# Attention in a hybrid decoder layer: q projected from consecutive tokens and transposed straight into place, inverse roots by Ln, Exp and one Newton step

## The chip, the cores and the metric

The kernel runs on one core of one Trainium2 chip. The metric is the device time of one execution in microseconds; the kernel before has three runs, and their median is 2185.88 us. The engines are named as in the profile: PE is TensorE (PEld its weight loads), DVE is VectorE, ACT is ScalarE, POOL is GpSimd, and SP is SyncE, which here only issues DMAs.

## The reference, cut to what matters

One decoder layer over x of 2048 tokens by 1024 in float32. Eight attention heads of 64, each with three dilated windows whose results are mixed by their softmax denominators; a short convolution stands beside them; a SwiGLU follows.

```
h = rms_norm(x, g_mix);  z = h @ w_in
u, gb, gc, q, k, v = split(z)
y_conv = gb * short_conv(gc * u, conv_w)
q = rms_norm(q.reshape(B, S, 8, 64), g_q) * 64 ** -0.5
k = rms_norm(k.reshape(B, S, 8, 64), g_k)
y_attn = dilated_mixture(q, k, v)        # (window, dilation) = (128,1), (512,4), (2048,16)
mix = concat(rms_norm(y_conv), rms_norm(y_attn));  x = x + mix @ w_out
h = rms_norm(x, g_ffn);  x = x + (silu(h @ w_gate) * (h @ w_up)) @ w_down
```

The normalisation of q and k is what the change touches: each of 64 elements is multiplied by 1/sqrt(mean of squares + 1e-6).

## The kernel before, in words

Every matrix product is made in three float16 products, high by high, high by low and low by high, because each float32 operand is split into a high and a low half (mm3_steps, L182 to L190: three matmuls per chunk k of 128 contraction rows, eight chunks). The stages are: the input norm and three quarters of the convolution (in_and_conv), attention (attention_pairs), the output projection (out_b), the feed-forward (ffn).

Attention works on four pairs of heads, g = 0 to 3. For each pair, qkv_steps (L443 to L507) projects q, k and v of both heads, in blocks of 512 tokens (i), four tiles of 128 tokens (j) each. A tile takes every fourth token of its block (t = slice(j, 4 * P, 4), L461), as the layout of k and v wants it. The tile's matmuls have the tokens as stationary operand and 384 columns of weights moving: 128 of q, 128 of k, 128 of v. ACT copies q and k out of PSUM (L468), squares them (L469), and splits v with DVE (L472, L473). When four tiles are there, DVE sums the squares (L479) and makes the inverse root of 128x16 numbers by rsqrt (L39 to L51): a shift and a subtraction on the bits of the number as a first guess (L45, L46), three Newton rounds of three operations (L48 to L50), and a multiplication by 2^11 (L482). POOL multiplies q and k by it (L483, L486); ACT and POOL split them in high and low halves in one buffer, qkhl (L492 to L495). SP issues three transposing DMAs of 128x1024 (L499 to L502): one for q into the scratch qp, two for k into ka and kl. Since the tokens of a tile are four apart, DVE copies q from qp into token order in qT (L503 to L505), one copy of 128x512 per head.

attn_steps (L509 to L651) runs the three branches of both heads over qT, ka and kl: matmuls of q against k in high and low (L606, L607), mask and row minimum on DVE (L612), Exp on ACT (L617), a split into halves (L627, L628), a transposing DMA of the weights (L629) or, where only one block of keys is seen, a transposition on PE (L622 to L624), and the product with v (L635). POOL combines the three branches of a head (combine, L536 to L559).

What sets the order: attention_pairs (L707 to L727) weaves the projection of pair g+1, or in the last pair the remaining quarter of the convolution and the first part of the output projection (tail_steps), between the steps of attention g, so many projection steps per attention step (rate) and not before the product with v some steps back (lag, issue_after). A projection step is one yield: three matmuls, or the end of a block. The framework then orders the instructions of each engine by a simulated timeline and puts in all semaphores. Each engine, and SP's queue of DMAs, works in that order, so an instruction that waits holds all behind it. The first pair's projection (qkv_steps(0)) has no attention beside it until its first block is done.

Buffers: the pool qk has four buffers of 4 KB per partition under the name qT. Two are used for the heads of a pair; in the convolution they serve as w1 (L301), in the input norm for tiles 6 and 7 (L393), in the output projection (out_a, L781) for the residual tiles x1 of two rows of tokens, where p is not 1, 4 or 7. The names ka and kb have two buffers of 8 KB each.

Of the kernel before, what the change touches and what calls it, by code (L numbers as in the profile page):

```python
# [2 lines left out]

# [5 lines left out]
F32 = mybir.dt.float32  # L9
F16 = mybir.dt.float16  # L10
I32 = mybir.dt.int32
AF = mybir.ActivationFunctionType
ALU = mybir.AluOpType
# [4 lines left out]
P = 128  # L18
S = 2048
D = 1024  # L20
# [5 lines left out]
HD = 64  # L26
EPS = 1e-6


class Builder:  # L30
# [167 lines left out]
    def run(self):  # L198
        tc, nc, A = self.tc, self.nc, self.A
        with ExitStack() as ctx:  # L200
            cp = ctx.enter_context(tc.tile_pool(name="const", bufs=1))
            self.cp = cp
            dr = self.dr = ctx.enter_context(tc.tile_pool(name="dram", bufs=1, space=DRAM))
            self.d_ya = dr.tile([P, 4, S], F32, name="d_ya")
            self.d_v = [dr.tile([2, S, 2 * HD + 2], F16, name=f"d_v{g}") for g in range(4)]
            self.d_u = [[dr.tile([S, HD + 2], F32, name=f"d_u{h}_{b}") for b in range(2)] for h in range(H)]
            self.d_wq = [dr.tile([P, 2, KC, 384], F16, name=f"d_wq{g}") for g in range(5)]
            self.d_wo = [dr.tile([P, 2, KC, 512], F16, name=f"d_wo{g}") for g in range(2)]
            self.d_y = dr.tile([S, 512], F32, name="d_y")
            self.d_x1 = dr.tile([S, D], F32, name="d_x1")  # L210
            self.d_h = dr.tile([S // 2, 7, 2 * 512], F16, name="d_h")
            self.d_wd = [dr.tile([P, NF // 2, 2, 512], F16, name=f"d_wd{n}") for n in range(7)]
            self.d_a = dr.tile([P, NF, S], F32, name="d_a")

            self.ident32 = cp.tile([P, P], F32, name="ident32")
            self.ones = cp.tile([P, 1], F32, name="ones")
            self.eps = cp.tile([P, 3], F32, name="eps")
            self.wsm = ctx.enter_context(tc.tile_pool(name="wsm", bufs=3))
            self.big = ctx.enter_context(tc.tile_pool(name="big", bufs=1))
            self.wq = ctx.enter_context(tc.tile_pool(name="wq", bufs=2))  # L220
            with ExitStack() as c1:
                e = c1.enter_context
                self.psmm = e(tc.tile_pool(name="psmm", bufs=3, space=PSUM))
                self.qk = e(tc.tile_pool(name="qk", bufs=4))
                self.mixer(c1)

                self.fs = ctx.enter_context(tc.tile_pool(name="fs", bufs=1, side="right"))
                self.fw = ctx.enter_context(tc.tile_pool(name="fw", bufs=15, side="right"))

                self.gs = ctx.enter_context(tc.tile_pool(name="gs", bufs=2, side="right"))  # L230
                self.psg = ctx.enter_context(tc.tile_pool(name="psg", bufs=4, space=PSUM, side="right"))
                self.out_b()
            self.ffn()
# [36 lines left out]
    def conv_steps(self, j, W, before=None, scratch=None):  # L270


        nc, wc = self.nc, self.wc
        NC = 512
        prev = None
        two = {}
# [6 lines left out]
        for c in range(S // NC):  # L283
            if before:
                before(c)
            t = slice(c * NC, (c + 1) * NC)
# [11 lines left out]
                return ps, u  # L298
            gc, u = yield from gemm(2)
            own = scratch if c == 0 else None  # L300
            w1 = own[:, 0:2] if own is not None else self.qk.tile([P, 2, NC], F32, name="qT")  # L301
            gcs, a = w1[:, 0], w1[:, 1]
            nc.scalar.activation(gcs, gc, AF.Copy, scale=u)
            yield True
# [14 lines left out]
            y, s2 = w2[:, 0], w2[:, 1]  # L319
# [5 lines left out]
            acc = self.sq[:, c] if j < 3 else s2  # L325
            if j == 0:
                s2 = acc
            nc.scalar.activation(s2, y, AF.Square)
            if 0 < j < 3:
                nc.gpsimd.tensor_tensor(acc, acc, s2, op=ALU.add)  # L330
                s2 = acc
# [33 lines left out]
    def in_and_conv(self):  # L365
        tc, nc, A = self.tc, self.nc, self.A
        w_in, w_out = A["w_in"][0], A["w_out"][0]
        with ExitStack() as c:
# [21 lines left out]
                W[m] = self.weights([cols(0)[m]], ux, dst=(t0[:, 0, :, cs], t0[:, 1, :, cs]), raw=raw0[:, m])  # L390

            def norm(i, n):
                tags = 6 * ("nx_x",) + ("qT", "qT") + 8 * ("nx_x",)  # L393
                self.norm(i, [(self.qk if tg != "nx_x" else xp).tile([P, D], F32, name=tg) for tg in tags[i:i + n]],
                          [t[:, j] for tg in ("ka", "kb")[i % 4 // 2:(i % 4 + n) // 2]
                           for t in (self.qk.tile([P, 2, 2, D], F16, name=tg, bufs=2),) for j in range(2)])
            spills = []
# [45 lines left out]
    def qkv_steps(self, g, st):  # L443
# [5 lines left out]
        u = self.uq[:, g:g + 1]  # L449
        st["u"] = u  # L450
        yield
        qT = [self.qk.tile([P, S], F16, name="qT") for _ in range(2)]

        ka, kl = (self.qk.tile([P, 4, 2, 512], F16, name=nm, bufs=2) for nm in ("ka", "kb"))
        dv = self.d_v[g]
        for i in range(0, NT, 4):
            f = self.at.tile([P, 4, 4, HD], F32, name="qkf", bufs=2)
            for j in range(4):
                vs = self.vs[i // 4 % 2]

                t = slice(j, 4 * P, 4)  # L461
                xh, xl = self.x[i // 4]
                ps = self.psmm.tile([P, 512], F32, name="mm")
                yield from self.mm3_steps(ps[:, 0:384], lambda k: xh[:, k, t], lambda k: xl[:, k, t],
                                          lambda k: wh[:, k], lambda k: wl[:, k])
                if j == 0:
                    n = self.at.tile([P, 16, HD], F32, name="qkn")
                nc.scalar.activation(f[:, j].rearrange("p a b -> p (a b)"), ps[:, 0:256], AF.Copy, scale=u)  # L468
# [8 lines left out]
            ff = f.rearrange("p a b d -> p (a b) d")  # L477
            ss = self.at.tile([P, 16], F32, name="qk_ss")
            nc.vector.tensor_reduce(ss, n, axis=AX.X, op=ALU.add)  # L479
            nc.vector.tensor_scalar(ss, ss, 1.0 / HD, EPS, op0=ALU.mult, op1=ALU.add)  # L480
            r = self.rsqrt(self.at, ss, 16, "qkr")
            nc.vector.tensor_scalar_mul(r, r, 2.0 ** 11)  # L482
            nc.gpsimd.tensor_tensor(n, ff, r.unsqueeze(2).broadcast_to([P, 16, HD]), op=ALU.mult)  # L483
            n4 = n.rearrange("p (a b) d -> p a b d", a=4)
            nk = n4[:, :, 2:4]
# [9 lines left out]
                nc.gpsimd.tensor_tensor(hl[:, 4 + h, :, 0], k, hl[:, 2 + h, :, 0], op=ALU.subtract)  # L495


            qp = self.at.tile([P, 2, 4, P], F16, name="qp", bufs=2)
            for n_, dst in enumerate((qp, ka[:, i // 4].rearrange("p h (j t) -> p h j t", j=4),  # L499
                                      kl[:, i // 4].rearrange("p h (j t) -> p h j t", j=4))):  # L500
                self.transpose(dst.rearrange("p h j t -> p (h j) t"),
                               hl[:, 2 * n_:2 * n_ + 2].rearrange("p h j x d -> p (h j x d)"))  # L502
            for h in range(2):  # L503
                nc.vector.tensor_copy(qT[h][:, i * P:(i + 4) * P].rearrange("p (t j) -> p t j", j=4),
                                      qp[:, h].rearrange("p j t -> p t j"))  # L505
            yield
        st.update(qT=qT, ka=ka, kl=kl)  # L507

    def attn_steps(self, g, st):  # L509
# [16 lines left out]
                for r in range(4):  # L526
                    nc.sync.dma_start(t[32 * r:32 * r + 32], dv.rearrange("(n p r) c -> r p n c", n=NT, r=4)[r])
        for h, b in [(h, b) for h in range(2) for b in (1, 2, 0)]:
            qT = st["qT"][h]
            ka, kl = (st[x][:, :, h] for x in ("ka", "kl"))  # L530
            load_v(h, b)

# [134 lines left out]
    def attention_pairs(self):  # L667
# [27 lines left out]
        nc.vector.tensor_scalar_mul(self.kap, u, HD ** -0.5 * 2.0 ** -22)  # L695
        nc.vector.tensor_scalar_mul(self.nkap, self.kap, -1.0)

        self.qkhl = self.at.tile([P, 6, 4, 2, HD], F16, name="qkhl")
        nc.gpsimd.memset(self.qkhl[:, 4:6, :, 1], 0.0)
        self.y7 = self.rows.tile([P, NT, HD], F32, name="y7")  # L700
# [61 lines left out]
    def out_a(self, p):  # L762
# [5 lines left out]
            ya = tk[:, 0].rearrange("p a (b c) -> p (a b) c", c=2 * P).rearrange("p k (j t) -> p k j t", j=2)  # L768
        else:
            ya = self.op.tile([P, 4, 2, P], F32, name="ya")  # L770
        xk = self.qk.tile([P, 2, D], F32, name="kb", bufs=2) if p % 3 == 1 else None
        for j in range(2):
            nc.sync.dma_start(ya[:, :, j], self.d_ya[:, :, (p + 8 * j) * P:(p + 8 * j + 1) * P])
        for k in range(4):
# [3 lines left out]
        self.x1[p] = []  # L778
        for j in range(2):
            i = p + 8 * j  # L780
            x1 = self.qk.tile([P, D], F32, name="qT") if xk is None else xk[:, j]  # L781
            nc.sync.dma_start(x1, self.A["x"][0][i * P:(i + 1) * P])
            t = tk[:, 1, j] if p < 2 else self.op.tile([P, 512], F32, name="xt", bufs=2)

# [436 lines left out]
```

## Time and profile before

| what | value |
|---|---|
| three runs | 2181.43, 2185.88, 2189.73 us; median 2185.88 |
| span of the profiled execution | 2189.4 us; the run of 2189.73 is the one that fits it, 0.3 around the span |
| PE busy over the span | 2068.8 us, 94% |
| DVE, ACT, POOL busy | 1457.8 (67%), 1025.1 (47%), 625.8 us (29%) |
| mean granted clock of PE | 0.984 |
| loads of ACT's function table | 5 |

Matmuls are pipelined, so PE counts as busy also where the next one starts only as the last one's results arrive; what a matmul costs is read from the distance of two starts, not from its length. A row of a timeline gives start, length, engine, line, operation, the tile written and those read, the shape, and in brackets the idle time before it and what ended it. A row of waits gives who waited, for whom, the microseconds in total, how often, and the longest. A row of groups gives busy time, the mean in ns, and the idle time before.

### The profile page before, as it was taken

The page shows a single profiled execution, that of the slowest core. Times are in us where ns is not written, and L with a number is a line of the kernel's source. Part 1 is how long each engine was busy: PE and PEld are TensorE (multiplying, and loading weights), DVE is VectorE, ACT ScalarE, POOL GpSimd, SP SyncE. Part 2 cuts the span into 40 slices and gives each one's busy share as a digit, 9 for nine tenths or more (in the row PEclk, how much of TensorE's full clock was granted, in tenths as well). Part 3 has the DMA queues.
Part 4 walks back from the last instruction along what each step waited for, and adds up shares of the span by engine and source line. Part 5 has one row for each costly group of instructions (what it writes and reads, how often), then busy time and mean ns, then how long its engine had stood idle before and what let it go on. Part 6 is the DMA issues. An engine that isn't in the chain of part 4 may idle for free. (4 is left out here: it accounts for less than half of the span.)

```text
span 2189.4 us, 32832 instructions
## 1 busy us (share of the span) xinstructions
PE 2068.8 (94%) x11864; PEld 1077.2 (49%) x11864; DVE 1457.8 (67%) x3380; ACT 1025.1 (47%) x2134; POOL 625.8 (29%) x515
## 2 busy tenths in 40 slices
PE   4899999989899889999999999999999999999999
PEld 2344567767666544443444444444444444444444
DVE  5687446778776687795767676756676666545554
ACT  6443346776766656563433333333333334444341
POOL 0000133343443212120232111211121145555463
PEclk9999999999999989999999999999999999999999
DMA  9767458899989996799332233223322663251342
GB/s 245 169 201 243 115 119 153 186 178 178 183 168 202 208 214 216 242 276 263 124 109 87 97 106 101 89 95 101 106 87 97 235 241 105 77 180 54 119 142 96
DMA packets 555492, 339.64 MB, mean 155 GB/s; under 512 B 354624, under 2 KB 508224, under 8 KB 552896
## 3 DMA queue, kind: packets, MB, share of 16 engines
q1 hardware_dynamic: 537648, 314.38, 55.9%
q10 hardware_dynamic: 17680, 23.16, 3.0%
q8 instruction: 93, 1.52, 0.3%
q14 instruction: 71, 0.58, 0.1%
HBM read 161.24 MB, written 107.54 MB: 123 GB/s over the span
## 5 line engine op out<-in xcount | busy, mean ns | idle before, releaser
L1001 PEld LDWEIGHTS <-w 128*128 128x128 f16 x3696 | 362.3, 98 | 454.9 <-issue 20.2
L1001 PE MATMUL ps<-b,w 128*128 128x512 f16 x2112 | 466.5, 382 | 14.0 <-DVE s L1007 6.1
L1132 PE MATMUL ps<-b,w 128*128 128x512 f16 x1848 | 399.8, 379 | 4.0 <-DVE s L1153 2.2
L1001 PE MATMUL ps<-hb,w 128*128 128x512 f16 x1584 | 347.1, 379 | 0.0
L1132 PEld LDWEIGHTS <-w 128*128 128x128 f16 x1848 | 180.8, 98 | 222.9 <-issue 5.4
L187 PE MATMUL mm<-wq,b 128*128 128x384 f16 x512 | 171.8, 335 | 7.1 <-DVE vs L473 7.1
L894 POOL TENSOR_TENSOR t<-wq 128x512 f32<-128x512 f32 (+1 forms) x46 | 59.5, 1294 | 411.4 <-issue 239.0
L1007 DVE TENSOR_TENSOR s<-ps,s 128x512 f32<-128x512 f32 x220 | 150.0, 683 | 34.4 <-PE ps L1001 33.9
L189 PE MATMUL mm<-wq,b 128*128 128x384 f16 x512 | 171.7, 335 | 0.0
L188 PE MATMUL mm<-wq,b 128*128 128x384 f16 x512 | 171.5, 335 | 0.0
L1139 POOL TENSOR_TENSOR x<-x,s 128x512 f32<-128x512 f32 x72 | 103.4, 1436 | 172.6 <-DVE s L1153 134.2
L1140 DVE SCALAR_TENSOR_TENSOR x<-ps,a_u,x 128x512 f32<-128x512 f32 x96 | 71.8, 749 | 100.9 <-PE ps L1132 74.3
L617 ACT ACTIVATE s<-s,u 128x256 f32<-128x256 f32 (+1 forms) x224 | 97.9, 452 | 69.4 <-DVE u L612 50.2
L612 DVE CUSTOM_DVE_ANT_0 s<-s,mask,nkap 128x256 f32<-128x256 f32 (+1 forms) x224 | 104.6, 483 | 19.5 <-PE s L607 13.9
L188 PEld LDWEIGHTS <-b 128*128 128x128 f16 x768 | 84.5, 110 | 67.1 <-issue 18.2
L187 PEld LDWEIGHTS <-b 128*128 128x128 f16 x768 | 84.4, 110 | 61.5 <-ACT b L775 6.4
L911 ACT CAST w<-t 128x512 f16<-128x512 f32 x88 | 53.7, 616 | 127.4 <-PE ps L1001 61.9
L189 PEld LDWEIGHTS <-b 128*128 128x128 f16 x768 | 84.2, 110 | 57.2 <-issue 5.2
L187 PE MATMUL cvx<-b,wq 128*128 128x512 f16 (+1 forms) x200 | 77.0, 388 | 32.1 <-ACT kb L264 24.8
L635 PE MATMUL av<-v,et 128*128 128x65 f16 x1800 | 77.7, 195 | 28.1 <-DMA et<-eh 18.7
L606 PE MATMUL s<-ka,qT 128*128 128x128 f16 (+1 forms) x408 | 91.8, 272 | 10.3 <-DVE eh L628 9.2
L1120 DVE TENSOR_TENSOR w<-t,w 128x512 f16<-128x512 f32 (+1 forms) x96 | 75.3, 801 | 34.2 <-ACT w L1119 33.9
(297 smaller groups left out, 3773.4 us busy)
## 6 DMA issues: line engine op xcount, KB each, us to landing
d_a<-a ACTq DMA_DIRECT2D x88, 256.0 KB, 2.0
d_wd<-w SPq DMA_DIRECT2D x77, 256.0 KB, 2.1
wq<-d_a SPq DMA_DIRECT2D x64, 256.0 KB, 4.2
b<-d_wd SPq DMA_DIRECT2D x14, 1024.0 KB, 6.3
wraw<-in_w_in_dram SPq DMA_DIRECT2D x24, 512.0 KB, 7.2
d_h<-hl SPq DMA_DIRECT2D x24, 512.0 KB, 3.2
wq<-in_w_gate_dram SPq DMA_DIRECT2D x22, 512.0 KB, 5.3
wq<-in_w_up_dram SPq DMA_DIRECT2D x22, 512.0 KB, 5.2
```

What stands on the lines that cost most here:

```text
L187: self.pe = mm(ps, lhsT=lh(k), rhs=rh(k), start=k == ks[0], stop=False)
L188: mm(ps, lhsT=lh(k), rhs=rl(k), start=False, stop=False)
L189: mm(ps, lhsT=ll(k), rhs=rh(k), start=False, stop=k == ks[-1])
L606: nc.tensor.matmul(o, lhsT=query(u), rhs=hi[x], start=True, stop=False)
L612: nc.vector.tensor_tensor_reduce(sm[:, at[u]], sp[:, at[u]], mask[:, P - P * has_prev(u):256], accum_out=Ub[:, u, HD + 1:HD + 2], op0=ALU.add,
L617: nc.scalar.activation(sm[:, at[u]], sm[:, at[u]], AF.Exp, scale=-1.0, bias=Ub[:, u, HD + 1:HD + 2])
L635: self.pe_av = nc.tensor.matmul(av[:, u - u0], lhsT=p_, rhs=v_, start=n_ == 0, stop=n_ == len(ops) - 1)
L1001: nc.tensor.matmul(ps[self.BANK[n]], lhsT=w[:, x, k], rhs=b[:, y, k], start=first and k == 0 and q == 0, stop=k == 3 and q == 2, skip_grou ...
L1007: nc.vector.tensor_tensor(t, x, y, op=ALU.add)
L1120: nc.vector.tensor_tensor(L[n][:, 1, 0:n_f], src[n], L[n][:, 0, 0:n_f], op=ALU.subtract)
L1132: nc.tensor.matmul(ps[self.BANK[n]], lhsT=L[n][:, x, f], rhs=B[n][:, f, y], start=first and f == 0 and q == 0, stop=f == n_f - 1 and q == ...
L1139: nc.gpsimd.tensor_tensor(o, o, s_, op=ALU.add)
```

## The change

Five edits. (1) A tile's k and v are still projected from every fourth token, with 256 columns moving; q is projected by 24 matmuls of its own, of 128 columns, from 128 consecutive tokens, into the same PSUM tile and without yields between them. (2) Its transposes, one per head and of half the size, go straight into qT; the scratch qp and DVE's copies are gone. (3) The inverse root comes from Ln and Exp on ACT and one Newton round on DVE. (4) The table set that has Ln and Exp is loaded after the last square of the third convolution quarter. (5) The qT buffers become two of 8 KB, each for both heads, or for pairs of the other uses.

```diff
-                self.qk = e(tc.tile_pool(name="qk", bufs=4))
+                self.qk = e(tc.tile_pool(name="qk", bufs=2))
...
-            w1 = own[:, 0:2] if own is not None else self.qk.tile([P, 2, NC], F32, name="qT")
+            w1 = own[:, 0:2] if own is not None else pair(c, "qT").rearrange("p (a b) -> p a b", a=2)
...
-        qT = [self.qk.tile([P, S], F16, name="qT") for _ in range(2)]
-
+        qT = self.qk.tile([P, 2, S], F16, name="qT")
...
-                t = slice(j, 4 * P, 4)
                 xh, xl = self.x[i // 4]
                 ps = self.psmm.tile([P, 512], F32, name="mm")
-                yield from self.mm3_steps(ps[:, 0:384], lambda k: xh[:, k, t], lambda k: xl[:, k, t],
-                                          lambda k: wh[:, k], lambda k: wl[:, k])
+                t, tq = slice(j, 4 * P, 4), slice(j * P, (j + 1) * P)
+                yield from self.mm3_steps(ps[:, 128:384], lambda k: xh[:, k, t], lambda k: xl[:, k, t],
+                                          lambda k: wh[:, k, 128:384], lambda k: wl[:, k, 128:384])
+                self.mm3(ps[:, 0:128], lambda k: xh[:, k, tq], lambda k: xl[:, k, tq],
+                         lambda k: wh[:, k, 0:128], lambda k: wl[:, k, 0:128])
...
+            r = self.at.tile([P, 16], F32, name="qkr_y")
+            t = self.at.tile([P, 16], F32, name="qkr_t")
+            nc.scalar.activation(t, ss, AF.Ln, scale=1.0 / HD, bias=self.lnb[:, 0:1])
+            nc.scalar.activation(r, t, AF.Exp, scale=-0.5, bias=self.lnb[:, 1:2])
             nc.vector.tensor_scalar(ss, ss, 1.0 / HD, EPS, op0=ALU.mult, op1=ALU.add)
-            r = self.rsqrt(self.at, ss, 16, "qkr")
-            nc.vector.tensor_scalar_mul(r, r, 2.0 ** 11)
+            nc.vector.scalar_tensor_tensor(t, r, -0.5 * 2.0 ** -22, r, op0=ALU.mult, op1=ALU.mult)
+            nc.vector.tensor_tensor(t, t, ss, op=ALU.mult)
+            nc.vector.scalar_tensor_tensor(r, t, 1.5, r, op0=ALU.add, op1=ALU.mult)
...
-            qp = self.at.tile([P, 2, 4, P], F16, name="qp", bufs=2)
-            for n_, dst in enumerate((qp, ka[:, i // 4].rearrange("p h (j t) -> p h j t", j=4),
-                                      kl[:, i // 4].rearrange("p h (j t) -> p h j t", j=4))):
-                self.transpose(dst.rearrange("p h j t -> p (h j) t"),
+            for h in range(2):
+                self.transpose(qT[:, h, i * P:(i + 4) * P].rearrange("p (j t) -> p j t", j=4),
+                               hl[:, h].rearrange("p j x d -> p (j x d)"))
+            for n_, dst in ((1, ka), (2, kl)):
+                self.transpose(dst[:, i // 4].rearrange("p h (j t) -> p (h j) t", j=4),
                                hl[:, 2 * n_:2 * n_ + 2].rearrange("p h j x d -> p (h j x d)"))
-            for h in range(2):
-                nc.vector.tensor_copy(qT[h][:, i * P:(i + 4) * P].rearrange("p (t j) -> p t j", j=4),
-                                      qp[:, h].rearrange("p j t -> p t j"))
...
+        with self.tc.issue_after(self.sqr.ins):
+            nc.scalar.preload_act_table_set("natural_log_exp_and_others")
+        self.lnb = self.at.tile([P, 2], F32, name="lnb")
+        nc.vector.memset(self.lnb[:, 0:1], EPS)
+        nc.vector.memset(self.lnb[:, 1:2], 11 * math.log(2.0))
...
-        xk = self.qk.tile([P, 2, D], F32, name="kb", bufs=2) if p % 3 == 1 else None
+        xk = self.qk.tile([P, 2, D], F32, name="kb" if p % 3 == 1 else "qT")
...
-            x1 = self.qk.tile([P, D], F32, name="qT") if xk is None else xk[:, j]
+            x1 = xk[:, j]
```

The lines left out give the last square of the convolution a name (self.sqr, L328), give the input norm's tiles 6 and 7 one buffer, and let the attention read its head's half of qT.

More of the change, by code (lines that the diff above doesn't have):

```diff
@@ L2 @@
 from itertools import chain, islice
+import math
 import concourse.bass as bass
@@ L327, in conv_steps @@
                 s2 = acc
-            nc.scalar.activation(s2, y, AF.Square)
+            self.sqr = nc.scalar.activation(s2, y, AF.Square)
             if 0 < j < 3:
@@ L392, in norm @@
             def norm(i, n):
-                tags = 6 * ("nx_x",) + ("qT", "qT") + 8 * ("nx_x",)
-                self.norm(i, [(self.qk if tg != "nx_x" else xp).tile([P, D], F32, name=tg) for tg in tags[i:i + n]],
+                two = self.qk.tile([P, 2, D], F32, name="qT") if i <= 6 < i + n else None
+                self.norm(i, [two[:, k - 6] if k in (6, 7) else xp.tile([P, D], F32, name="nx_x") for k in range(i, i + n)],
                           [t[:, j] for tg in ("ka", "kb")[i % 4 // 2:(i % 4 + n) // 2]
@@ L528, in attn_steps @@
         for h, b in [(h, b) for h in range(2) for b in (1, 2, 0)]:
-            qT = st["qT"][h]
+            qT = st["qT"][:, h]
             ka, kl = (st[x][:, :, h] for x in ("ka", "kl"))
```

## The prediction

> **What bounds the kernel now.** I read the table of stages first, then the chain of waits by engine, then the timeline around each wait that TensorE (PE) has in the attention stage.
>
> ```profile
> 307.00:690.00 383.00, 349.60 (x3383) 263.20 (x3382) 280.87 (x1009) 259.06 (x693) 148.73 (x115) 0.96 0.92 179
> ...
> 1045.00:2189.00 1144.00, 1130.89 (x5230) 511.29 (x5228) 722.67 (x1237) 430.01 (x764) 382.28 (x299) 1.00 0.35 116
> ```
>
> The columns are stretch, length, busy time of PE, of PE's weight loads, of DVE, ACT and POOL, granted clock, DMA share, GB/s. The feed-forward stage, 1144 us from 1045 on, has PE busy for 1130.89 and is not touched. The change acts in the 383 us from 307 to 690, where attention of one pair of heads runs beside the projection of the next; the first projection stands ahead of it. PE is busy there for 349.60, so at most some 33 us can be won from waiting. Who ends these waits:
>
> ```profile
> PE s L606 <- DVE eh L628: 8.9, 6, 2.6
> PE av L635 <- DMA et<-eh: 7.9, 12, 2.0
> PE mm L187 <- DVE vs L473: 6.9, 5, 2.2
> ```
>
> ```profile
> DVE qT L504 <- DMA qp<-qkhl: 15.8, 9, 5.9
> ```
>
> Eleven waits, 15.8 us, are for DVE. Another 7.9 us are for the DMA transposes of the softmax weights. DVE, in its turn, stood for 15.8 us in front of the copy of q (L504), with everything queued behind it.
>
> **What the change removes: the copy.** The timeline where PE waited for DVE (the brackets hold the idle time before the instruction):
>
> ```profile
> 617.67 4.92 DVE L504 COPY qT<-qp 128x512 f16<-128x512 f16 x2 [0.19 <-DMA qp<-qkhl]
> ...
> 623.65 0.37 PE L606 MATMUL s<-ka,qT 128*128 128x256 f16 x1 [2.57 <-DVE eh L628]
> ```
>
> ```profile
> 353.23 0.32 PE L187 MATMUL mm<-wq,b 128*128 128x384 f16 x1 [0.55 <-DVE vs L473]
> ...
> 429.49 0.32 PE L187 MATMUL mm<-wq,b 128*128 128x384 f16 x1 [1.12 <-DVE vs L473]
> ...
> 504.33 0.37 PE L606 MATMUL s<-ka,qT 128*128 128x256 f16 x1 [2.14 <-DVE eh L628]
> ...
> 562.89 0.27 PE L606 MATMUL s<-ka,qT 128*128 128x256 f16 x1 [0.74 <-DVE eh L628]
> ```
>
> Followed back step by step, each of these five stalls leads over the softmax's DVE and ACT steps, or over L473 alone, to a copy L504. At 617.67 two copies took 4.92 us, against 29.9 us for all 32 (below). The five stalls are 0.55 + 1.12 + 2.14 + 0.74 + 2.57 = 7.1 us. The copies go, and nothing else was queued before those DVE steps, so I take all of it: **-7.1 us**; between -4 (the next late transpose takes over) and -7.1.
>
> **What the change removes: the root's DVE steps.**
>
> ```profile
> L504 DVE COPY qT<-qp 128x512 f16<-128x512 f16 x32 | 29.9, 976 | 19.3 <-DMA qp<-qkhl 19.2
> ...
> L50 DVE SCALAR_TENSOR_TENSOR qkr_y<-qkr_t,qkr_y 128x16 f32<-128x16 f32 x48 | 10.6, 222 | 1.1
> ```
>
> ```profile
> 569.29 2.16 DVE L46 TENSOR_SCALAR qkr_y<-qkr_i 128x16 int32<-128x16 int32 x1
> ...
> 572.80 0.28 PE L606 MATMUL s<-ka,qT 128*128 128x128 f16 x1 [2.45 <-DVE eh L628]
> ```
>
> ```profile
> 448.45 0.53 PE L635 MATMUL av<-v,et 128*128 128x65 f16 x12 [1.81 <-ACT u L638]
> ```
>
> Thirteen DVE operations of 128x16 per block of 512 tokens become four: L45, L46, two of three rounds of L48 to L50 and L482 go. At L50's mean of 0.222 us, nine are 2.0 us per block, 32 us over the 16 blocks, and the copies are 29.9: 62 us of DVE time, which costs PE only where DVE is late. Two stalls, 2.45 + 1.81 = 4.3 us, lead back to such a step drawn out to about 2 us (L46 at 569.29 is one; why, the rows don't say). Four steps stay that can be drawn out likewise, so I take half: **-2.2 us**, between 0 and -4.3.
>
> **What it adds on PE.** Each of the 64 tiles had 24 matmuls of 384 columns; it gets 24 of 256 and 24 of 128, each with a weight load of its own: 1536 more. Starts in one stretch:
>
> ```profile
> 435.34 0.22 PE L607 MATMUL s<-kb,qT 128*128 128x128 f16 x1
> 435.40 0.27 PE L606 MATMUL s<-ka,qT 128*128 128x256 f16 x1
> 435.50 0.27 PE L607 MATMUL s<-kb,qT 128*128 128x256 f16 x1
> 435.61 0.27 PE L606 MATMUL s<-ka,qT 128*128 128x256 f16 x1
> ...
> 435.83 0.33 PE L187 MATMUL mm<-wq,b 128*128 128x384 f16 x1
> 436.00 0.33 PE L188 MATMUL mm<-wq,b 128*128 128x384 f16 x1
> ```
>
> ```profile
> 402.31 0.30 PE L607 MATMUL s<-kb,qT 128*128 128x128 f16 x1
> 402.44 0.30 PE L606 MATMUL s<-ka,qT 128*128 128x128 f16 x1
> ```
>
> From start to start: 384 columns take about 0.163 us, 256 take 0.108, 128 take about 0.056 where the moving operand is contiguous (435.34) and 0.13 where both operands step (402.31). All had their weight load hidden or paid within that. The new q matmuls have both operands contiguous, and the stationary tokens of k and v step by four as qT does at 435.34, so I take the first: 0.108 + 0.056 - 0.163 = 0.001 to 0.002 us, times 1536: **+2.5 us**. The bounds are -1 (rounding) and 1536 x 0.074 = +114.
>
> The Trainium skill, "TensorE: Matmul & The Clock Gate", section "Back-to-back issue gap", speaks against the change: it puts a sustained stream of weight load and 128-column matmul at about 81 ns each, which would make this term 1536 x 0.026 = 40 us, an estimate from that page. The rows from 435.34 on do not agree; they stand in short runs, though, and the new ones are runs of 24.
>
> **What it adds on SP's queue.** Three transposes per block become four, the two of q half as large.
>
> ```profile
> L195 SPq DMA_TRANSPOSE qp<-qkhl x16: 1232/1292/2314, 268.7 to 667.1; - x16
> ```
>
> Issuing one took SP 1.29 us in the median. Twelve of the 16 blocks lie beside attention: 12 x 1.29 = 15.5 us more of SP in 383. Queued behind are the transposes of the softmax weights, for which PE already waits. Half size may be cheaper to issue; no row shows it. If one in three lands on a transpose that PE waits for, it is +5; freed DVE writes those weights earlier, up to -8. I take **+1**.
>
> **What it adds on ACT.** Ln and Exp on 128x16, nearest:
>
> ```profile
> L546 ACT ACTIVATE cw<-cw 128x48 f32<-128x48 f32 (+1 forms) x11 | 2.7, 241 | 8.5 <-DVE cw L545 8.4
> ```
>
> ```profile
> 286.85 1.28 ACT L617 ACT_TABLE_LOAD   x1
> ```
>
> 2 x 0.24 x 12 = 5.8 us on an engine busy 259.06 of 383; that alone is hidden by its idle time. But Ln waits on ACT for DVE's sum, DVE's next step waits for Exp, and ACT's evacuations and exponentials queue behind Ln, as DVE's masks queue behind that step: **+1**, 0 to +12. The table load, 1.28 us once, moves ahead of attention, where PE had other work: 0.
>
> **What the paired buffers add.** Two buffers of 8 KB replace four of 4 KB. The orders of reuse come out equal, but both halves of a pair are released together.
>
> ```profile
> 888.09 1.14 ACT L858 ACTIVATE ka<-qT,n_y 128x1024 f32<-128x1024 f32 x1
> ...
> 894.94 0.59 PE L187 MATMUL mm<-b,b 128*128 128x512 f16 x1 [4.29 <-DVE qT L788]
> ```
>
> In the output stage a load of x into such a buffer waits for L858; the first half now waits for the second's 1.14 us as well, at three places, of which one stalls PE today: **+1.1**, 0 to +3.4.
>
> The sum: -7.1 - 2.2 + 2.5 + 1 + 1 + 1.1 = **-3.7 us**. The profiled span is 2189.4; one of the three runs is 2189.73, 0.3 around it, and the median of the three, 2185.88, is 3.5 below the span. So 2185.7 for such an execution, **2182 us** for the median.
>
> **Rivals.** Half a percent, 11 us, is about what a measurement of this kernel can tell from no change.
>
> First, DVE's relief reaches the transposes too. For it: 62 us less on DVE, and DVE feeds every transpose. Against: several of those stalls lead back to PE itself and to a long transfer. With all 11.4 us of the DVE stalls and the 7.9 us for the transposes gone, and the costs of 5.6: -13.7 us, so 2172. Chance 0.29.
>
> Second, slower: the wait for the copy comes back as the round trip to ACT. Place: DVE's step behind Exp, and ACT behind Ln, in 12 blocks. The old wait of 15.8 us and copies of up to 29.9 cost PE 7.1, some 0.2 us for each us that DVE stood or copied. ACT and DVE now stand both; with 2.5 us each per block, 60 us in all, PE loses 12: 2182 + 12 = 2194. It passes 2197, and so decides, from about 3.2 us per block. ACT's longest such wait is in the row below, its mean 1.5.
>
> ```profile
> ACT s L617 <- DVE u L612: 43.9, 29, 5.7
> ```
>
> Chance 0.09.
>
> Third, slower: weight loads set the pace of the 128-column matmuls. At midway between 0.056 and 0.13 it is 1536 x 0.037 = 57 us, and 2182 + 57 = 2239; it decides from 0.066 us a matmul. Chance 0.04; the page's 81 ns lies in this case.
>
> Fourth, the change doesn't do what it says: Ln and Exp do not share the loaded table set, and each block loads twice, 32 x 1.28 = 41 us on ACT, some 16 us at PE: 2198. The Trainium skill, "ScalarE: Activation LUTs", section "Table sets: the hidden batching unit", has both functions in the set that is named; no run here shows it yet. Chance 0.03.
>
> **How the numbers follow.** Within 0.5%: 0.55, with an own range from 2175, where the DVE stalls go whole and the costs are near zero, to 2193, where ACT's term is at its end. Faster: 0.29, the first rival. Slower: 0.16, the last three, 0.09 + 0.04 + 0.03. The range leaves out about 0.1 on either side: from 2165 (the first rival with the terms of ACT, SP and the buffers at zero, 2169, less half the 8 us over which the three runs spread) to 2198 (the second at 2.5 us, 2194, and the same half; the table loads give as much).
>
> **What would show it.** Right: no wait of DVE for q's transposes; the five stalls gone; 128-column L187 to L189 starting 0.056 apart; five table loads; PE's waits for transposes as before. Wrong: DVE waiting for ACT at the Newton step or ACT at Ln by over 3 us a block; q's matmuls over 0.066 apart; SP's longer queue showing as more waits for the softmax transposes; or these waits shrinking by more than half.

## The result, and the profile after

| kernel | median of its four runs | ratio to before, 95% interval |
|---|---|---|
| before | 2186.85 us (2181.43 to 2189.73) | 1 |
| the change | 2173.64 us (2171.84 to 2177.16) | 0.9944 [0.9929, 0.9959] |

The change is 13.2 us faster. The interval lies wholly below 1, so there is a gain; whether it is more or less than 0.5% is not settled, as 0.995 lies inside the interval. The forecast was 2182 us; the result lies inside its range, and next to the 2172 us of its first rival.

The profiled execution has a span of 2170.0 us (the run of 2171.84) against 2189.4. The table of stages of the changed kernel, over the stretch of attention that was shown of before, and a stretch of the feed-forward as long as the one shown:

```profile
307.00:690.00 383.00, 355.44 (x4677) 328.91 (x4676) 249.02 (x901) 274.54 (x740) 149.69 (x115) 1.00 0.97 187
...
1026.00:2170.00 1144.00, 1134.72 (x5252) 513.60 (x5249) 724.65 (x1238) 429.85 (x764) 382.38 (x299) 1.00 0.35 117
```

The feed-forward is as it was. In attention the DVE column fell from 280.87 to 249.02 us, and the granted clock, 0.96 before, is 1.00. To see all of attention, here is the stretch from its first product with v to its last, 479.4 us before:

```profile
323.90:803.30 479.40, 435.01 (x4212) 317.92 (x4212) 355.90 (x1307) 316.83 (x841) 160.55 (x119) 0.95 0.94 186
```

and 460.3 us after:

```profile
323.10:783.40 460.30, 425.25 (x5317) 370.93 (x5317) 311.71 (x1167) 326.00 (x874) 157.08 (x118) 0.98 0.98 192
```

The 19.1 us between these two are the whole difference of the two spans, 19.4. PE idled 479.40 - 435.01 = 44.4 us before and 460.30 - 425.25 = 35.1 us after: 9.3 us. The other 9.8 us are busy time of PE, although it runs 1105 matmuls more; the granted clock beside them is 0.98 where it was 0.95. Who ended PE's waits in the first stretch of the changed kernel, and the one wait of ACT that the change added:

```profile
PE av L640 <- DMA et<-eh: 17.8, 21, 2.5
...
PE s L611 <- DVE eh L633: 2.5, 5, 1.0
```

```profile
ACT qkr_t L484 <- DVE qk_ss L481: 7.0, 6, 1.5
```

The waits for DVE, 8.9 + 6.9 us before, are down to 2.5, and the longest is 1.0. But the wait of the product with v for the transposed softmax weights has grown from 7.9 to 17.8 us, where "as before" was forecast. Part of that is the stretch, which ends at 690 us in both kernels, while the changed one is further on by then: over all of attention, 307 to 790 us, the two are 18.7 and 22.7 us (the rows stand under e1 and e2).

The new operations, from the table of groups (busy us, mean ns, idle before):

```profile
L485 ACT ACTIVATE qkr_y<-qkr_t,lnb 128x16 f32<-128x16 f32 x16 | 5.1, 322 | 0.4
L484 ACT ACTIVATE qkr_t<-qk_ss,lnb 128x16 f32<-128x16 f32 x16 | 5.1, 321 | 10.6 <-DVE qk_ss L481 10.4
L487 DVE SCALAR_TENSOR_TENSOR qkr_t<-qkr_y 128x16 f32<-128x16 f32 x16 | 4.0, 247 | 0.7 <-ACT qkr_y L485 0.7
```

the q matmuls of one tile, the first two and the last of 24, and the next tile's first matmul of k and v, from PE's timeline:

```profile
349.62 0.22 PE L188 MATMUL mm<-wq,b 128*128 128x128 f16 x1
349.68 0.22 PE L189 MATMUL mm<-wq,b 128*128 128x128 f16 x1
...
350.91 0.22 PE L190 MATMUL mm<-wq,b 128*128 128x128 f16 x1
350.96 0.27 PE L188 MATMUL mm<-wq,b 128*128 128x256 f16 x1
```

and q's transposes on SP's queue (minimum, median and maximum ns of issuing one):

```profile
L196 SPq DMA_TRANSPOSE qT<-qkhl x32: 1188/1223/2569, 270.8 to 664.1; - x32
```

### The profile page after: what moved, and what is told of

Its sections match the earlier page's. It is cut to its first block, busy times and chain, and to the rows that moved or that the text cites. A ratio compares the mean times of both kernels' runs of the same rounds, so it can differ in the third digit from the quotient of the medians.

```text
span 2170.0 us, 35813 instructions
## 1 busy us (share of the span) xinstructions
PE 2063.9 (95%) x13400; PEld 1153.8 (53%) x13400; DVE 1407.3 (65%) x3206; ACT 1033.2 (48%) x2166; POOL 626.2 (29%) x515
## 4 chain that ended last, share of the span: by engine, by line
PE 44%; DVE 2%; DMA 2%; ACT 1%; POOL 1%; issue 1%; SPq 0%; ACTq 0%; DVEq 0%; POOLq 0%
PE ps L1011 29%; PE ps L1142 15%; DMA wq<-d_a 1%; ACT wq L1120 0%; DVE w L1130 0%; ACT wq L941 0%; DVE w L922 0%; DMA wq<-in_w_up_dram 0%; DMA wq<-in_w_gate_dram 0%; POOL x L1149 0%; ACT w L1129 0%; DVE s L1017 0%; POOL t L904 0%; DVE w L925 0%; DMA wq<-in_w_down_dram 0%
## 5 line engine op out<-in xcount | busy, mean ns | idle before, releaser
L1011 PEld LDWEIGHTS <-w 128*128 128x128 f16 x3696 | 362.6, 98 | 452.8 <-issue 17.4
L1011 PE MATMUL ps<-b,w 128*128 128x512 f16 x2112 | 466.4, 381 | 12.3 <-DMA b<-d_h 4.6
L189 PE MATMUL mm<-wq,b 128*128 128x256 f16 (+1 forms) x1024 | 233.7, 248 | 0.0
L188 PE MATMUL mm<-wq,b 128*128 128x256 f16 (+1 forms) x1024 | 231.5, 248 | 0.0
L190 PE MATMUL mm<-wq,b 128*128 128x256 f16 (+1 forms) x1024 | 231.3, 248 | 0.0
L189 PEld LDWEIGHTS <-b 128*128 128x128 f16 x1280 | 134.4, 105 | 36.6 <-issue 5.9
L188 PEld LDWEIGHTS <-b 128*128 128x128 f16 x1280 | 134.3, 105 | 36.6 <-ACT b L785 4.9
L190 PEld LDWEIGHTS <-b 128*128 128x128 f16 x1280 | 134.1, 105 | 31.6 <-issue 0.8
L622 ACT ACTIVATE s<-s,u 128x256 f32<-128x256 f32 (+1 forms) x224 | 98.8, 456 | 28.8 <-DVE u L617 20.0
L640 PE MATMUL av<-v,et 128*128 128x65 f16 x1800 | 80.3, 195 | 27.1 <-DMA et<-eh 22.7
L633 DVE TENSOR_TENSOR eh<-s,eh 128x512 f16<-128x512 f32 (+1 forms) x112 | 75.2, 678 | 42.3 <-ACT eh L632 42.1
L1043 ACT ACTIVATE sg<-s,w_un 128x512 f32<-128x512 f32 x66 | 47.2, 719 | 105.2 <-DVE s L1017 105.2
```

What stands on the lines that cost most here:

```text
L188: self.pe = mm(ps, lhsT=lh(k), rhs=rh(k), start=k == ks[0], stop=False)
L189: mm(ps, lhsT=lh(k), rhs=rl(k), start=False, stop=False)
L190: mm(ps, lhsT=ll(k), rhs=rh(k), start=False, stop=k == ks[-1])
L622: nc.scalar.activation(sm[:, at[u]], sm[:, at[u]], AF.Exp, scale=-1.0, bias=Ub[:, u, HD + 1:HD + 2])
L633: nc.vector.tensor_tensor(eh[:, w:2 * w], sm[:, 0:w], eh[:, 0:w], op=ALU.subtract)
L640: self.pe_av = nc.tensor.matmul(av[:, u - u0], lhsT=p_, rhs=v_, start=n_ == 0, stop=n_ == len(ops) - 1)
```

## The experiments

Twelve kernels ran. Ratios are against the kernel before on the same chip; its medians there were 2185.87 us for the first four, 2187.15 for the next four, 2186.38 for the three after, and 2186.57 for the last.

| kernel | median us | ratio, 95% interval | DVE busy us |
|---|---|---|---|
| e1 q part alone | 2203.12 | 1.0078 [1.0065, 1.0091] | 1437.9 |
| e2 root alone | 2173.59 | 0.9943 [0.9926, 0.9960] | 1425.7 |
| e3 change, q in one stream with k and v | 2174.34 | 0.9944 [0.9931, 0.9957] | 1407.2 |
| e4 change, q's matmuls spread | 2184.00 | 0.9987 [0.9973, 1.0000] | 1412.9 |
| e5 before, later order | 2195.32 | 1.0048 [1.0025, 1.0071] | 1458.0 |
| e6 change, later order | 2191.59 | 1.0034 [1.0018, 1.0051] | 1406.8 |
| e7 q part alone, later order | 2202.02 | 1.0069 [1.0044, 1.0093] | 1435.6 |
| e8 root alone, later order | 2176.08 | 0.9958 [0.9939, 0.9978] | 1423.5 |
| e9 root alone and nine idle DVE steps | 2196.34 | 1.0057 [1.0036, 1.0078] | 1492.6 |
| e10 before, q transposed by head | 2182.08 | 0.9980 [0.9965, 0.9996] | 1453.1 |
| e11 change with two waiting copies | 2191.56 | 1.0023 [1.0010, 1.0036] | 1453.7 |
| e12 change with two copies that don't wait | 2192.26 | 1.0022 [1.0008, 1.0036] | 1458.8 |

The first theory, C, was that the copy of q and DVE's wait in front of it were most of the gain. Its rivals, as they came up: D, that DVE's occupied time is what counts, whichever step fills it; T, that the shorter chain from the sum of squares to POOL's multiplication counts; S, that the fourth transpose on SP's queue takes something back. The texts put on record before the runs name some others: R, that the root is the gain; W and L, that the added matmuls or their standing in one lump are what the q part pays; O, that the order of the instructions moves the time as much as the change does, against M, that it doesn't.

**The two parts alone (e1, e2).** e1 is the kernel before with edits 1, 2 and 5 of the change (q projected apart, transposed by head, no copy, paired buffers) and the old root. e2 is the kernel before with edits 3 and 4 alone:

```diff
+            nc.scalar.activation(t, ss, AF.Ln, scale=1.0 / HD, bias=self.lnb[:, 0:1])
+            nc.scalar.activation(r, t, AF.Exp, scale=-0.5, bias=self.lnb[:, 1:2])
...
-            r = self.rsqrt(self.at, ss, 16, "qkr")
-            nc.vector.tensor_scalar_mul(r, r, 2.0 ** 11)
+            nc.vector.scalar_tensor_tensor(t, r, -0.5 * 2.0 ** -22, r, op0=ALU.mult, op1=ALU.mult)
+            nc.vector.tensor_tensor(t, t, ss, op=ALU.mult)
+            nc.vector.scalar_tensor_tensor(r, t, 1.5, r, op0=ALU.add, op1=ALU.mult)
```

> The q part of the change alone (own matmuls for q, transposes straight into qT, no copy, paired buffers), with the inverse root made on DVE as before. Theory C (the copy with its wait for the transpose held DVE, and most of the gain is that DVE is free of it): most of the 13 us, 2175 to 2179, no wait of DVE for q's transposes, few of PE for L628 and L473. Rival R (the shorter root is what counts, the copy was hidden): 2183 or more.

> The root part alone (Ln, Exp, one Newton round, the table loaded ahead), with q projected beside k and v, transposed into the scratch and copied as before. Theory C: 2182 to 2187, DVE still waits some 15 us for q's transposes. Rival R: 2176 to 2180. A third possibility, that the two only help together because either alone leaves DVE late: both e1 and e2 at 2182 or more.

Theory C fell at once, and R held in kind, though e2 is faster than R's 2176 to 2180. The root alone gives the whole gain, 0.9943; the q part alone, with no copy and no wait in front of it, is 17 us slower than before. PE's waits over all of attention (307 to 790 us), first of before:

```profile
PE av L635 <- DMA et<-eh: 18.7, 19, 3.0
PE s L606 <- DVE eh L628: 9.2, 7, 2.6
PE mm L187 <- DVE vs L473: 6.9, 5, 2.2
```

of the q part alone:

```profile
PE av L635 <- DMA et<-eh: 34.8, 36, 2.9
PE s L606 <- DVE eh L628: 7.3, 6, 5.2
...
PE mm L188 <- DVE vs L475: 1.6, 3, 0.8
```

of the root alone:

```profile
PE av L641 <- DMA et<-eh: 23.1, 17, 4.1
...
PE s L612 <- DVE eh L634: 1.2, 2, 1.0
```

and of the change:

```profile
PE av L640 <- DMA et<-eh: 22.7, 24, 3.1
...
PE s L611 <- DVE eh L633: 2.9, 6, 1.0
```

Read the rows of one kernel together: L628 writes eh, the split of the softmax weights, and the transposes et carry eh to the product with v. One chain, and PE waits now for its one end, now for the other. The sums are 34.8 us before, 43.7 for the q part alone, 24.3 for the root alone and 25.6 for the change, and the times of these four stand nearly in that order: 2186, 2203, 2174, 2174. The sum is no measure of the time by itself, though: e3 below has 29.5 + 4.7 = 34.2 us and 2174, e11 17.4 + 11.0 = 28.4 us and 2192. The q part took 7.2 us from the waits for DVE and gave 16.1 back at the transposes.

**What of the q part gives it back (e3, e4).** e3 is the change with q projected in one stream of 384 columns with k and v; q then comes out in the order of k's tokens, so the reordering is left out. e4 is the change with two chunks to a step: the matmuls of k and v fill the first four of the tile's eight steps, q's 24 the last four.

```diff
-                yield from self.mm3_steps(ps[:, 128:384], ...)
-                self.mm3(ps[:, 0:128], ...)
+                yield from self.mm3_steps(ps[:, 0:384], lambda k: xh[:, k, t], lambda k: xl[:, k, t],
+                                          lambda k: wh[:, k], lambda k: wl[:, k])
```

```diff
-                yield from self.mm3_steps(ps[:, 128:384], ...)
-                self.mm3(ps[:, 0:128], ...)
+                both = chain(self.mm3_steps(ps[:, 128:384], ...), self.mm3_steps(ps[:, 0:128], ...))
+                for _ in both:
+                    next(both)
+                    yield
```

> The changed kernel, but q projected in one stream of 384 columns with k and v from every fourth token, as before; its transposes still go straight into qT. This puts q's tokens in another order than the reference's within each block of 512, so it leaves the reordering out. It takes away the 1536 added matmuls and weight loads alone. Prediction's term (2.5 us): 2170 to 2173 beside 2174 for the change. Rival W (weight loads or the lump of 24 matmuls without a yield cost more): 2165 or less.

> The changed kernel with q's 24 matmuls spread over the same eight steps as those of k and v (two chunks of matmuls per step) in place of a lump at the end of a tile. If the lump delays attention's own matmuls: 2 to 6 us below the change, with fewer waits of PE for the softmax transposes. If not: within 3 us of 2174.

Without the split stream e3 takes 2174.34 us, the change 2173.64: the 1536 added matmuls cost nothing that can be measured here, nor does the lump, which e3 takes away with them, and W falls. e4 made it worse, 2184.00, so yields between q's matmuls don't bring the loss back; it isn't a clean test of the lump, since it packs the matmuls of k and v twice as densely too. Both kernels also fall into other orders, and both times lie outside what either theory had given. The waits of the product with v in e3:

```profile
PE av L638 <- DMA et<-eh: 29.5, 24, 4.8
```

and in e4:

```profile
PE av L643 <- DMA et<-eh: 34.5, 29, 2.3
```

Both are above the change's 22.7.

**Another order (e5 to e8).** The same four kernels (before, change, q part, root) with the projection's steps held back by one step of attention more:

```diff
-            rate, lag = (4.52, 3.49, 3.2, 2.1)[g], (12, 12, 13, 8)[g]
+            rate, lag = (4.52, 3.49, 3.2, 2.1)[g], (13, 13, 14, 9)[g]
```

> The kernel before with every lag one step longer (13, 13, 14, 9): the same work in another order on each engine. It is the base of a second set of four, for the same two parts. Theory O (the order that the framework's simulated timeline happens to give moves the time by as much as the change does): 6 us or more away from 2186 on either side. Rival M (the parts themselves act, order is small): within 4 us of 2186.

> The changed kernel with the same longer lags. Theory O: its distance to the kernel before with these lags differs from the 12 us measured by 6 us or more. Rival M: 9 to 15 us below that kernel.

> The q part alone with the same longer lags. Theory M: 17 us or so above the kernel before with these lags, as with the old ones. Theory O: its last pair of heads is no longer 13 us longer than that of the kernel before, and the distance shrinks below 8 us.

> The root part alone with the same longer lags. Theory M: 9 to 15 us below the kernel before with these lags. Theory O: anything from level to 20 us below; in both, the stretch of the first three pairs should be some 4 us or more shorter than in that kernel, if the shorter root itself helps.

Theory O holds: e6 is 4 us below e5, where the change was 13 below before; e7 is 7 above, where e1 was 17; e8 is 19 below, where e2 was 12. The root still gains in every pair of kernels that differ by it alone: before to e2 -12, e1 to the change -29, e5 to e8 -19, e7 to e6 -10 us. The q part never gains: before to e1 +17, e2 to the change 0, e5 to e7 +7, e8 to e6 +16 us. The later order itself is worth -1 to +18 us. So a single pair of kernels says little about an edit of this size here: the order that it falls into is worth as much as the edit.

**DVE's time or the chain (e9).** The new root on the kernel before, and behind it nine DVE operations of 128x16 per block, on a scratch that nothing reads:

```diff
+            w = self.at.tile([P, 16], F32, name="qkr_w")
+            nc.vector.tensor_scalar(w, ss, 1.0, 0.5, op0=ALU.mult, op1=ALU.add)
+            for _ in range(4):
+                nc.vector.scalar_tensor_tensor(w, w, -0.5, w, op0=ALU.mult, op1=ALU.mult)
+                nc.vector.tensor_tensor(w, w, ss, op=ALU.mult)
```

> The root part alone, and nine more DVE operations of 128x16 per block of 512 tokens on a scratch that nothing reads, started when the root is ready: as many as the new root saves, but off the chain from the sum of squares to q and k. Theory D (the saved DVE work itself is the gain, since each small operation can hold up the softmax): back towards the kernel before, 2183 or more. Rival T (the shorter chain, from sum to root about 4 us in place of 9, is the gain): 2172 to 2177.

The chain of the root, from the end of the sum of squares to POOL's multiplication, stayed short: 4.01 us in the mean of the last twelve blocks, 4.20 in e2, 8.80 before. Yet the time rose by 22.7 us over e2. Theory T falls as the cause, and D stands, as far as one run in one order can tell. PE's wait:

```profile
PE s L617 <- DVE eh L639: 20.3, 11, 6.0
```

The added groups, and where the longest of their members lie in the timeline:

```profile
L492 DVE SCALAR_TENSOR_TENSOR qkr_w<-qkr_w 128x16 f32<-128x16 f32 x64 | 39.0, 609 | 1.0
L493 DVE TENSOR_TENSOR qkr_w<-qkr_w,qk_ss 128x16 f32<-128x16 f32 x64 | 36.7, 574 | 1.1
```

```profile
442.60 1.98 POOL L494 TENSOR_TENSOR qkn<-qkf,qkr_y 128x1024 f32<-128x1024 f32 x1 [17.48 <-DVE qkr_w L493]
442.73 1.88 DVE L492 SCALAR_TENSOR_TENSOR qkr_w<-qkr_w 128x16 f32<-128x16 f32 x1
...
444.54 3.81 POOL L561 TENSOR_TENSOR r<-r,cw 128x1040 f32<-128x1040 f32 x2
...
444.64 1.85 DVE L493 TENSOR_TENSOR qkr_w<-qkr_w,qk_ss 128x16 f32<-128x16 f32 x1
...
446.82 1.56 DVE L492 SCALAR_TENSOR_TENSOR qkr_w<-qkr_w 128x16 f32<-128x16 f32 x1
...
449.85 0.37 PE L617 MATMUL s<-ka,qT 128*128 128x256 f16 x1 [4.92 <-DVE eh L639]
```

Add start and length: the DVE step of 442.73 ends at 444.61, the POOL operation of 442.60 at 444.58. The next DVE step ends at 446.49, the first of the two POOL operations in the row of 444.54 at 446.46 (the row merges two); the third at 448.38, the second of the two at 448.35. Three steps whose median length is 0.175 us, and whose results nothing reads, hold DVE for 5.3 us; 1.5 us later PE goes on, after 4.92 us of waiting for eh. (The bracket of the first row names the DVE step that ended last before POOL went on; POOL reads qkr_y, which none of the added steps writes.)

**SP's queue (e10).** The kernel before with q transposed by head, four transposes per block; the copies stay.

```diff
-            for n_, dst in enumerate((qp, ka..., kl...)):
+            for h in range(2):
+                self.transpose(qp[:, h], hl[:, h].rearrange("p j x d -> p (j x d)"))
+            for n_, dst in ((1, ka...), (2, kl...)):
```

> The kernel before, with q's transpose into the scratch made as one per head (four DMAs per block in place of three), copies and all else kept. Theory S (the added transpose on SP's queue is what the q part pays): PE's waits for softmax transposes grow from 19 us towards 35, and the time by 5 us or more, 2191 to 2203. Rival L (the reordered matmuls and the lump of q's 24 are what it pays): within 4 us of 2186.

2182.08 us, 0.998 [0.9965, 0.9996]: in this order the fourth transpose costs nothing, and S falls: PE waited 17.6 us for the softmax transposes between 307 and 790 us, 18.7 before. The same run speaks against C, too. DVE's wait in front of the copies of q was 19.2 us before. In e10, from the view of the tile qp (who waited for it: us, times):

```profile
DVE qT L506: 46.1, 21
```

27 us more of DVE standing before a copy, and a time no longer. Only some 9.5 of them are beside attention (25.3 us from 307 us on, 15.8 before); the rest stand ahead of it.

**Copies put back (e11, e12).** The change, with two copies of 128x512 per block onto a scratch that nothing reads. In e11 they read the transposed q and so wait for its transposes; in e12 they read the split q from the buffer that the transposes read, and need no transfer.

```diff
+                nc.vector.tensor_copy(qp[:, h].rearrange("p j t -> p t j"), qT[:, h, i * P:(i + 4) * P].rearrange("p (j t) -> p t j", j=4))
```

```diff
+                nc.vector.tensor_copy(qp[:, h].rearrange("p j t -> p t j"), hl[:, h].rearrange("p j x d -> p (x d) j"))
```

> The changed kernel, with DVE's two copies per block put back onto a scratch that nothing reads; they wait for q's transposes as the old ones did. The prediction's term: 7 us more, 2181. If the copy's stalls were only handed on to the waits for the softmax transposes: within 3 us of 2174.

> The change with the same two DVE copies of 128x512 per block as in the kernel with the waiting copies, onto the same scratch that nothing reads, but read from the normalised q ahead of its transposes, so that they wait for no transfer. If it is DVE's occupied time that costs (30 us more on DVE, the copies' own 0.5 to 2.7 us each drawn out beside POOL), the time is near that kernel's, 2183 to 2194. If it is DVE standing in front of a copy whose transpose isn't there (20.2 us in 14 waits there), the time is the change's or little more, 2170 to 2179. Between 2179 and 2183 both have a part.

e11 is 18 us slower than the change, and so is e12, by 19: 2191.56 and 2192.26. For e11 both expectations, 2181 and near 2174, were too low; e12 is where D put it. In e11 DVE waited for the transposes, here from 307 to 790 us:

```profile
DVE qp L513 <- DMA qT<-qkhl: 20.2, 14, 3.7
```

In e12 that wait cannot be. There the copies themselves are long, and they waited for POOL's split of q instead:

```profile
L513 DVE COPY qp<-qkhl 128x512 f16<-128x512 f16 x32 | 54.2, 1827 | 15.2 <-POOL qkhl L501 15.2
```

So the loss needs no transfer to wait for. Of the 15.2 us of e12's wait for POOL, 12.3 lie ahead of 307 us and 2.9 beside attention, against e11's 20.2 there, and the time is the same. It isn't shown that waiting costs nothing: in e12 POOL is held too, with 43.7 us for its second subtraction (L502) against 21.7 in the change, so the two differ by more than the wait.

**A price for DVE's time.** Three pairs differ in the program by added DVE operations alone; the busy line of the page of the changed kernel, of e2, e9, e11 and e12:

```profile
PE 2063.9 (95%) x13400; PEld 1153.8 (53%) x13400; DVE 1407.3 (65%) x3206; ACT 1033.2 (48%) x2166; POOL 626.2 (29%) x515
```

```profile
PE 2062.1 (95%) x11864; PEld 1076.7 (50%) x11864; DVE 1425.7 (66%) x3238; ACT 1034.8 (48%) x2166; POOL 625.4 (29%) x515
```

```profile
PE 2071.4 (94%) x11864; PEld 1079.3 (49%) x11864; DVE 1492.6 (68%) x3382; ACT 1035.4 (47%) x2166; POOL 627.6 (29%) x515
```

```profile
PE 2069.1 (95%) x13400; PEld 1155.6 (53%) x13400; DVE 1453.7 (66%) x3238; ACT 1032.8 (47%) x2166; POOL 630.4 (29%) x515
```

```profile
PE 2069.5 (94%) x13400; PEld 1155.9 (53%) x13400; DVE 1458.8 (67%) x3238; ACT 1035.2 (47%) x2166; POOL 651.3 (30%) x515
```

e9 over e2: 66.9 us of DVE, 22.7 us of time, 0.34 per us. e11 over the change: 46.4 and 17.9, 0.39. e12: 51.5 and 18.6, 0.36. The root alone, the other way: 32.1 us of DVE off, 12.3 us of time, 0.38. DVE is busy two thirds of the span, and yet each added us of it comes with a third of a us and more.

Three things keep this from being a constant.

- The price differs by pair. The other pairs for the root give 0.36 (e7 to e6: 28.8 us of DVE, 10.4 of time), 0.56 (e5 to e8: 34.5 and 19.2) and 0.96 (e1 to the change: 30.6 and 29.5), and the q part takes 17 to 22 us off DVE and never gains.
- The added operations move the order of the others: counted in the traces without them, 259 of 3238 DVE instructions of e9 stand in another order than in e2, 153 of 3206 in e11 and 232 in e12 than in the change; the later order of e5 moves 291 of 3380, and that alone was worth some 8 us.
- About half of the gain doesn't stand where the DVE work was taken away. The last step of copy or root ends at 671.6 us before, at 655.2 in the change and 653.6 in e2. At the first product with v of the last pair, the change is 9.8 us ahead of before (679.3 against 689.1) and e2 11.6; at the end of attention they are 20 and 27 us ahead. The last pair's stretch, which holds no changed step, is 114.4 us before, 104.3 in the change, 99.2 in e2, and also 105.8 in e10, which spares DVE nothing worth counting.

So the sign of DVE's price is shown by seven pairs; its size is mixed with what the order does, and no run parts the two.

## Why the prediction was nearly right, and where it was wrong

The sign and the range held. The place (attention, PE's waits for DVE) held in part: these waits went, but half of the gain came in the last pair, most of which lies behind the stretch to 690 us that was read. The likeliest case, within 0.5%, was missed by a hair, 0.56%, and the size was too small: -3.7 us against -13.2. Term by term:

- **The copy, -7.1.** The five stalls went, as said: the longest wait for eh left is 1.0 us. But the term was sized by the stalls whose last link was a copy. At the price above, the 29.9 us of copies would be worth some 0.36 x 29.9 = 11 us (an estimate from e9, e11 and e12); what was measured of the q part as a whole, which takes the copies away, is no gain in any pair. e10 and e12 speak against the wait in front of the copies, which the prediction put first, as what costs.
- **The root, -2.2.** This is the step that failed. Two stalls that "lead back to such a step drawn out to about 2 us" were all that was counted, and half of them taken; the edit alone measures -12.3 (e2), and -10 to -29 in the other three pairs. The nine removed steps had been counted, 32 us, and rightly: the small steps of the root take 48.9 us before and 15.5 after. What failed was the rule that DVE time "costs PE only where DVE is late", read from the named stalls. Waits under other names and the granted clock moved with it; that DVE's lateness is passed on to them is the likely reading, not shown step by step. The prediction's own figure for its second rival, "some 0.2 us for each us that DVE stood or copied", would have given 62 x 0.2 = 12 us, near the 13.2, but by luck (its rows, 7.1 us over 45.7, make it 0.16): the root's 32 us alone would come to 6.4 where 12.3 was measured, and the copies to 6 where nothing came.
- **The split on PE, +2.5.** Right in kind: 24 q matmuls take 350.96 - 349.62 = 1.34 us, 0.056 each. In e3 the price can't be told from zero. The third rival (0.066 or more) is out; the page's 81 ns, from the Trainium skill, "TensorE: Matmul & The Clock Gate", section "Back-to-back issue gap", does not hold for these runs of 24.
- **SP's queue, +1.** Half size is hardly cheaper to issue, 1.22 us against 1.29, and four cost no more time than three in the one order tried (e10).
- **Ln and Exp on ACT, +1.** They take 0.32 us each, not 0.24. ACT waited 7.0 us in six waits at Ln between 307 and 690 us, 1.5 at most, DVE 0.7 us in all for Exp. The second rival needed 3.2 us per block. The table is loaded five times, at 1.24, 8.56, 245.70, 790.20 and 979.15 us, as often as before, so the fourth rival is out.
- **The paired buffers, +1.1.** The one stall is 4.3 us before and after: 0.
- **"PE's waits for transposes as before".** Wrong: 7.9 became 17.8 us in the stretch to 690, and 18.7 became 22.7 over all of attention. The first rival had the size, 2172, but by luck: its mechanism, relief that reaches the transposes, is wrong in the same way, as these waits grew.
- **The clock, at nothing.** The bound "at most some 33 us can be won from waiting" counts idle time alone, though the row it comes from has a clock of 0.96. Of the 19.1 us in attention, 9.8 are busy time of PE.

So, by these prices, two gains were too small by some 14 us together, and one cost was missing; that the sum still fell inside the range is in part luck. By the price of DVE's time the two parts should bring (48.9 - 15.5 + 29.9) x 0.36 = 23 us, an estimate; 13.2 came. What takes the rest back belongs to the q part: alone it is 17 us slower, and on top of the root it brings nothing. It shows at the softmax transposes. It doesn't look like the fourth transpose (e10), nor like the extra matmuls or their standing in one lump (e3), each tried in one order. The order into which the changed steps fall is worth as much (e5 to e8), but which of its moves costs is open.

The stall beside L46, where the prediction wrote "why, the rows don't say", can be read in one more row of the kernel before:

```profile
569.03 2.39 POOL L552 TENSOR_TENSOR u<-u,r 128x1040 f32<-128x1040 f32 x1
```

It ends at 571.42; L46, started at 569.29, ends at 571.45.

## What to carry to other kernels

Price an engine's time by the stage, and not by the stalls that end at its name: with this interleaved schedule a us of DVE cost a third of a us or more (0.34 to 0.96 over seven pairs), while the waits changed their names along the chain. Add up the waits of one chain before reading any of them, and try an edit of half a percent in a second order of the work before crediting it, since the order alone moved these kernels by up to 18 us. See also where a gain stands: half of this one came after the last step that the change had touched. Of a two-part change run each part alone first: here one part was the whole gain.

## What the runs showed of the hardware

The small DVE steps of the root are held, when they start inside a POOL operation, until it ends. Of the 208 steps of 128x16 of the root before, 11 took over 0.5 us, and all 11 began inside a POOL operation and ended within 0.04 us of its end; in e9 it is 56 of 208, all of them too. Of the others just one, before, began and ended inside a POOL operation. The held steps take 15.1 us before, 5.0 after (3 of 64), 66.9 in e9. The Trainium skill, "SBUF — State Buffer", section "Who interferes with whom", states it as a lock: a DVE instruction with two inputs in SBUF, or in a mode that uses both ports, and a GpSimd instruction that reads SBUF exclude each other for the whole of the one that came first. These traces agree but for that one step, and give the price: 0.17 us become up to 2.3.

About half of what the change gains in attention stands beside a higher granted clock. PE's timeline of the changed kernel around a wait:

```profile
437.82 0.54 PE L640 MATMUL av<-v,et 128*128 128x65 f16 x12 [2.54 <-DMA et<-eh]
...
440.02 0.31 PE L190 MATMUL mm<-wq,b 128*128 128x128 f16 x1
440.13 0.31 PE L188 MATMUL mm<-wq,b 128*128 128x128 f16 x1
```

and the granted clock there (the column behind POOL's), in stretches of 2 us:

```profile
436.00:438.00 2.00, 0.17 (x6) 0.18 (x7) 1.10 (x7) 0.14 (x1) 0.00 (x0) 1.00 0.87 192
438.00:440.00 2.00, 1.54 (x19) 1.15 (x16) 1.74 (x6) 1.94 (x6) 1.34 (x1) 0.58 1.11 224
```

After a wait of 2.54 us the matmuls of 128 columns start 0.107 us apart, where 0.056 is usual, and this lasts to 441.7. Inside attention there are nine such stretches before, 43.3 us in all, and two after, 17.1 us; at half speed they cost half their length, as far as PE is busy in them. In slices of 20 us from 300 to 800, ten of 25 have a clock below 1.00 before, three after. The root alone reaches the same time with six stretches and 30.7 us, so the clock's share differs from kernel to kernel. What follows a stall is in no row of waits, and the prediction, which counted waits alone, could not hold it. That the stall sets off the lower clock is read from their order here; no run tried it by itself, and a stall alone is not enough: waits of 2.73 us (ended at 555.51, the changed kernel) and 2.96 us (723.51, before) have no lower clock behind them.
